# Scores of an attention unit ordered behind the transposes, not the value products, two units back

## The chip, the cores and the metric

The kernel runs on one core of a Trainium2 chip, as one launch. The metric is device time in microseconds (us): the median of several executions. A profiled execution gives, besides its time, the span from its first to its last instruction and a record of every instruction on every engine: PE (TensorE, matmuls), PEld (its weight loads), DVE (VectorE), ACT (ScalarE), POOL (GpSimd), SP (SyncE, which issues the weight DMAs).

## What is computed

Two transformer blocks follow one another, for one sequence of 512 tokens and 1024 channels, in float32. The first block is FFN, a mixer of dilated attention and a gated recurrence, FFN. The second block is run for two layers, l = 0 and 1: a *hybrid mixer*, then a dense FFN (l = 0) or a mixture of eight experts (l = 1). Only the hybrid mixer, "the second kind of mixer", is touched. Its core, cut to what matters:

```
z = h @ w_in                      # q (8 heads), 3 pairs of k/v (2 groups), gates, u, bg, cg
o_cmp, p_cmp = cmp_attention(q, kc_c, vc_c)       # 31 compressed keys
o_sel = sel_attention(q, ks, vs, idx)             # 512 tokens are 8 blocks of 64, all chosen: causal
o_win = win_attention(q, kw, vw)                  # window of 512: causal
o_attn = g[0] * o_cmp + g[1] * o_sel + g[2] * o_win
o_conv = bg * conv3(cg * u)
return concatenate([o_attn, o_conv]) @ w_o
```

With 512 tokens both `o_sel` and `o_win` are plain causal softmax attention, so a mixer has 8 heads times 2 such branches.

## The kernel before

Every product in float32 is made of three matmuls on halves: a value is cut into a high and a low half (hi, lo), and hi*hi, hi*lo and lo*hi are summed (`mm3`, lines 429 to 431). Weights arrive by DMA as `w_raw`; ACT makes the high half (line 276), DVE and POOL share the low half (lines 280 and 282).

**A mixer** (`mix2`) has a main stream on TensorE: three projections by tokens (`tok_out`), two compressions of keys and values (`compress_mm`), six convolution jobs (`conv_out`, each 48 matmuls of 512 columns), and the convolution's part of the output projection (`out_proj`, 96 matmuls of 512 columns). Attention runs beside it as side streams, and after `flow.flush()`, which lets all of them come to their end, the attention's part of the output projection (`out_proj` again, with `closing`) follows.

**A unit** is one head (n) and one branch (br), u = 2n + br, 16 in a mixer. Its stages (`unit`, lines 925 to 1000):

- *scores*: four tiles of queries, two matmuls each (lines 948 and 949) into one of two `ps_s` banks; DVE adds the causal bias and takes the extreme (958), ACT exponentiates (960), DVE makes reciprocal and gate (963, 965), POOL scales (968). The results lie in three of six `ex` buffers.
- *transposes*: ten 128x128 transposes (980) into three `ps_t` banks, each bank cut by ACT and DVE (417, 418) into two of eight `pr` buffers.
- *value products* (PV): twelve matmuls into the head's `ps_o`, of which there is one bank. Both units of a head and its compressed branch (1571) add into it; after that it is cut into the `tok` operand of the output projection (417, 418).

`prep(n)` stacks and transposes a head's queries into one of four `q` pairs; `compressed(n)` does the compressed branch.

**The order** comes from a planner, `Flow`, which runs while the program is built: streams yield (cost on TensorE, delay until the stream may go on) or an `Event` to wait for; the main stream goes on step by step, and before each step every side stream that is due gets its turn. A planner's wait is no semaphore on the chip: it only decides in which order instructions are written down. For a unit the yields are

```
                yield 2 * mm_us(n), lag[2]       # a tile of scores; mm_us(512) is 0.215, lag[2] is 0
        yield 0.0, lag[0]                        # 9.75 from the last score to the first transpose
            yield 0.11 * off / P, lag[2]         # transposes of a bank: 3, 4 and 3 of them
        self.flow.mark(turned)
        yield 0.0, lag[1]                        # 5.18 from the last transpose to the value products
        for ev in before_pv:
            yield ev
            yield 3 * mm_us((4 - j) * P), 0.0    # value products, 1.78 in all
```

What was written down is then scheduled by the framework (`TileContext(..., schedule_with_timeline_sim=True)`): the order written is a priority, instructions whose operands or buffers are not there yet are passed over, and each engine in the end runs its own queue strictly in order, with semaphores put in by the framework.

Before, the planner starts the scores of unit u when the value products of u - 2 are done, and `prep(n)` when the compressed branch of head n - 2 is done.

Of the kernel before, what the change touches and what calls it, by code (L numbers as in the profile page):

```python
# [371 lines left out]
class Build:  # L372
# [988 lines left out]
    def mix2(self, norm, l, after):  # L1361
# [3 lines left out]
        with tc.tile_pool(name="m2_c", bufs=1) as mc, tc.tile_pool(name="m2_r", bufs=1) as rp:  # L1365
# [25 lines left out]
            ev = {n: Event() for n in ("k0", "k1", "q0", "q1", "g0", "g1", "wp0", "wp1", "kst", "vst")}  # L1391
# [102 lines left out]
            prepped = [Event() for _ in range(8)]  # L1494
            unit_done = [Event() for _ in range(16)]
            turn = [Event() for _ in range(16)]
            cmp_done = [Event() for _ in range(8)]
# [3 lines left out]
            def prep(n):  # L1501
                hd = order[n]
                if n > 1:
                    yield cmp_done[n - 2]
                yield ev["q%d" % (n // 4)]
                d = self.stacked(q[n // 4][hd // 4][:, :, hd % 2 * 64:hd % 2 * 64 + 64])
                yield 0.0, 3.11
                hds[n]["q"] = self.r(rp, S, "q"), self.r(rp, S, "q")
                self.cut(hds[n]["q"][0], hds[n]["q"][1], self.stack_rows(d))
                yield 0.44, 0.0  # L1510
                flow.mark(prepped[n], 6.18)

            def attend(n, br):
                hd, u = order[n], 2 * n + br
                g = hd // 4
                wait = [prepped[n], ev["k%d" % br], ev["g0"]] + ([unit_done[u - 2]] if u > 1 else [])
                before = [unit_done[u - 1]] if br else []
                lead = None
                if br:
                    wait.append(ev["kst"])  # L1520
                    p = self.t(P)
                    hds[n]["p"] = p

                    def lead(i, sc):
                        c = slice(i * 32, i * 32 + 32)
                        nc.vector.tensor_tensor(p[:, c], sc, cmp_bias[:, c], ALU.add)
                        if i == 0:
                            flow.mark(scored[n], 0.3)

                yield from self.unit(rp, hds[n], lambda: keys[br][g], causal, gates[:, :, br * 8 + hd],  # L1530
                                     lambda j: (vals[br][0][:, j], vals[br][1][:, j]),
                                     br == 0, False, wait, [turn[u - 1]] if u else [], turn[u], before,
                                     unit_done[u], None, lead)

            def compressed(n):
# [43 lines left out]
            for n in range(8):  # L1579
                flow.spawn(prep(n), 10 + 2 * n)  # L1580
                flow.spawn(attend(n, 0), 10 + 2 * n)
                flow.spawn(attend(n, 1), 11 + 2 * n)
                flow.spawn(compressed(n), 11 + 2 * n)
# [725 lines left out]
```

## Time and profile before

| | us |
|---|---|
| three runs: median (lowest to highest) | 2613.47 (2603.94 to 2617.77) |
| the profiled execution | 2615.04 |
| its span, first to last instruction | 2613.4 |
| second kind of mixer, l = 0: first unit's scores to last unit's PV | 1145.3 to 1347.6 |
| the same, l = 1 | 1820.0 to 2022.5 |

The profiled execution's time is 1.6 us over its span, and 1.6 us over the median of the three runs. All times below are us from the start of the span. A matmul's row shows its own duration, which overlaps the next one's: the distance from start to start is what it costs in a full stream.

### The profile page before, as it was taken

The numbers are of one execution on the slowest core, as the hardware profiler recorded it, in microseconds if no ns is written. First come the engines' busy times: TensorE is split into PE (matmuls) and PEld (weight loads), VectorE is DVE, ScalarE is ACT, GpSimd is POOL, SyncE is SP. The second block draws the span as 40 slices with busy tenths as digits, with TensorE's granted clock in tenths as the row PEclk, the third lists the DMA queues.
The fourth block names the chain that finished last, engine by engine and source line by source line (L and its number), as shares of the span: only waits on it lengthen the run. The fifth ranks groups of instructions, "written<-read, shape, count | busy, mean of one in ns | idle before, by whom it ended". The sixth has DMA issues, their size and how long they took to land. (4 is left out here: it accounts for less than half of the span.)

```text
span 2613.4 us, 39953 instructions
## 1 busy us (share of the span) xinstructions
PE 2520.9 (96%) x14307; PEld 2177.7 (83%) x14307; DVE 1622.0 (62%) x3324; ACT 1200.1 (46%) x2230; POOL 865.9 (33%) x885
## 2 busy tenths in 40 slices
PE   8999999999999999999999999999999998999996
PEld 6888889898888887898888888879888896978885
DVE  5424455768754344686775323358777577899886
ACT  4222235564532222455544222225555376777763
POOL 4222232322122222433233222243322116677630
PEclk9999999998999999999999999999999898999997
DMA  5734432212122322241112232232311298799892
GB/s 179 173 117 125 123 125 82 65 50 65 33 97 74 112 97 73 92 135 65 57 41 81 82 104 97 77 110 93 101 57 43 82 322 313 249 372 324 313 346 88
DMA packets 103883, 342.06 MB, mean 131 GB/s; under 512 B 11966, under 2 KB 12782, under 8 KB 103680
## 3 DMA queue, kind: packets, MB, share of 16 engines
q1 hardware_dynamic: 95616, 311.58, 35.1%
q0 software_dynamic: 8064, 27.87, 4.0%
q8 instruction: 115, 1.88, 0.3%
q14 instruction: 88, 0.72, 0.1%
HBM read 316.59 MB, written 22.81 MB: 130 GB/s over the span
## 5 line engine op out<-in xcount | busy, mean ns | idle before, releaser
L282 POOL TENSOR_TENSOR w_lo<-w_raw,w_hi 128x224 fp32r<-128x224 f32 (+3 forms) x542 | 615.5, 1140 | 1173.4 <-ACT w_hi L276 1093.5
L276 ACT CAST w_hi<-w_raw 128x1024 fp32r<-128x1024 f32 (+3 forms) x615 | 598.9, 982 | 827.1 <-issue 233.8
L280 DVE TENSOR_TENSOR w_lo<-w_raw,w_hi 128x800 fp32r<-128x800 f32 (+5 forms) x616 | 662.0, 1086 | 275.3 <-ACT w_hi L276 267.9
L430 PE MATMUL ps_mm<-act_lo,w_hi 128*128 128x512 f32 (+1 forms) x784 | 303.1, 387 | 1.3 <-DVE act_lo L418 1.3
L429 PE MATMUL ps_mm<-act_hi,w_hi 128*128 128x512 f32 (+1 forms) x784 | 304.1, 388 | 0.3 <-ACT act_hi L417 0.3
L431 PE MATMUL ps_mm<-act_hi,w_lo 128*128 128x512 f32 (+1 forms) x784 | 302.5, 386 | 0.0
L429 PE MATMUL ps_s<-act_hi,w_hi 128*128 128x512 f32 (+1 forms) x456 | 174.6, 383 | 7.0 <-ACT w_hi L279 6.6
L431 PE MATMUL ps_s<-act_hi,w_lo 128*128 128x512 f32 (+1 forms) x456 | 173.7, 381 | 1.1 <-DVE w_lo L280 1.1
L430 PE MATMUL ps_s<-act_lo,w_hi 128*128 128x512 f32 (+1 forms) x456 | 174.2, 382 | 0.0
L968 POOL TENSOR_SCALAR ex<-ex,st 128x512 f32<-128x512 f32 (+3 forms) x160 | 92.1, 588 | 246.5 <-DVE st L965 146.5
L431 PEld LDWEIGHTS ps_mm<-act_hi,w_lo 128*128 128x128 f32 x784 | 148.7, 190 | 29.0
L430 PEld LDWEIGHTS ps_mm<-act_lo,w_hi 128*128 128x128 f32 x784 | 148.2, 189 | 29.0 <-DVE act_lo L418 1.6
L429 PEld LDWEIGHTS ps_mm<-act_hi,w_hi 128*128 128x128 f32 x784 | 147.9, 189 | 28.0 <-ACT act_hi L417 0.3
L429 PE MATMUL ps_mm<-w_hi,act_hi 128*128 128x256 f32 (+1 forms) x544 | 157.4, 289 | 9.9 <-DVE nat L1259 5.6
L431 PE MATMUL ps_mm<-w_hi,act_lo 128*128 128x256 f32 (+1 forms) x544 | 156.3, 287 | 0.2 <-DVE act_lo L634 0.2
L430 PE MATMUL ps_mm<-w_lo,act_hi 128*128 128x256 f32 (+1 forms) x544 | 155.9, 287 | 0.0
L960 ACT ACTIVATE ex<-ex,st 128x512 f32<-128x512 f32 (+3 forms) x160 | 89.5, 560 | 65.4 <-DVE st L958 65.0
L429 PEld LDWEIGHTS ps_mm<-w_hi,act_hi 128*128 128x128 f32 x544 | 104.2, 191 | 11.9 <-DVE nat L1259 6.1
L429 PEld LDWEIGHTS ps_s<-act_hi,w_hi 128*128 128x128 f32 x456 | 86.4, 190 | 24.8 <-ACT w_hi L279 6.6
L430 PEld LDWEIGHTS ps_mm<-w_lo,act_hi 128*128 128x128 f32 x544 | 104.1, 191 | 0.9 <-DVE w_lo L280 0.5
L431 PEld LDWEIGHTS ps_mm<-w_hi,act_lo 128*128 128x128 f32 x544 | 103.9, 191 | 0.9 <-DVE act_lo L634 0.5
L431 PEld LDWEIGHTS ps_s<-act_hi,w_lo 128*128 128x128 f32 x456 | 86.8, 190 | 19.7 <-DVE w_lo L280 1.9
(700 smaller groups left out, 6305.1 us busy)
## 6 DMA issues: line engine op xcount, KB each, us to landing
w_raw<-ffn_a SPq DMA_DIRECT2D x131, 512.0 KB, 3.6
w_raw<-moe_x SPq DMA_DIRECT2D x128, 512.0 KB, 5.8
w_raw<-moe_a SPq DMA_DIRECT2D x88, 512.0 KB, 6.0
w_raw<-ffn_b SPq DMA_DIRECT2D x48, 384.0 KB
w_raw<-ffn_b SPq DMA_DIRECT2D x48, 320.0 KB, 2.8
w_raw<-m_conv SPq DMA_DIRECT2D x24, 512.0 KB, 3.7
w_raw<-moe_b SPq DMA_DIRECT2D x32, 384.0 KB, 4.4
w_raw<-win_n SPq DMA_DIRECT2D x20, 512.0 KB, 4.0
```

The costliest lines, as they stand in the source:

```text
L276: self.late(self.nc.scalar.copy(hi, src))
L280: self.nc.vector.tensor_tensor(lo[:, :n - m], src[:, :n - m], hi[:, :n - m].bitcast(F32), ALU.subtract)
L282: self.nc.gpsimd.tensor_tensor(lo[:, n - m:], src[:, n - m:], hi[:, n - m:].bitcast(F32), ALU.subtract)
L429: mm(out, l[0], r[0], start=first, stop=False)
L430: mm(out, l[0], r[1], start=False, stop=False)
L431: mm(out, l[1], r[0], start=False, stop=last)
L960: nc.scalar.activation(s, s, AF.Exp, bias=st[:, o:o + 1], scale=-1.0, accum_out=st[:, 2 + o:3 + o])
L968: nc.gpsimd.tensor_scalar(ex[i], ex[i], st[:, 4 + o:5 + o], 1.0, ALU.mult, ALU.mult)
```

## The change

Four waits of the planner are altered, and nothing else; no instruction, tile, buffer count or DMA is added or taken away.

```
             def prep(n):
                 if n > 1:
-                    yield cmp_done[n - 2]
+                    yield turn[2 * n - 3]
...
-                wait = [prepped[n], ev["k%d" % br], ev["g0"]] + ([unit_done[u - 2]] if u > 1 else [])
-                before = [unit_done[u - 1]] if br else []
+                wait = [prepped[n], ev["k%d" % br], ev["g0"]] + ([turn[u - 2]] if u > 1 else [])
+                order_t = ([turn[u - 1]] if u else []) + ([unit_done[u - 2]] if u > 1 else [])
+                before = [unit_done[u - 1]] if br else [cmp_done[n - 1]] if n else []
...
-                                     br == 0, False, wait, [turn[u - 1]] if u else [], turn[u], before,
+                                     br == 0, False, wait, order_t, turn[u], before,
                                      unit_done[u], None, lead)
```

`turn[u]` is marked when the transposes of unit u are written, `unit_done[u]` after its value products, `cmp_done[n]` after the compressed branch of head n. So scores of u wait for the transposes of u - 2; transposes of u wait for those of u - 1, as before, and now also for the value products of u - 2; the first value products of a head wait for the compressed branch of the head before; and a head's queries are prepared once the second unit of head n - 2 is transposed.

## Rows read from the trace of the kernel before

**Rows 1.** The page's first part: busy time (share of the span) xinstructions
```profile
PE 2520.9 (96%) x14307; PEld 2177.7 (83%) x14307; DVE 1622.0 (62%) x3324; ACT 1200.1 (46%) x2230; POOL 865.9 (33%) x885
```

**Rows 2.** Stretches: length; PE, PEld, DVE, ACT, POOL busy us; clock, DMA, GB/s
```profile
1145.00:1327.00 182.00, 181.51 (x1078) 159.11 (x1077) 135.47 (x410) 97.38 (x240) 57.00 (x82) 1.00 0.23 74
1327.00:1349.00 22.00, 20.98 (x134) 18.18 (x133) 15.04 (x50) 12.25 (x32) 4.88 (x9) 1.00 0.08 25
...
2002.00:2024.00 22.00, 18.47 (x118) 15.61 (x116) 15.66 (x56) 12.24 (x32) 5.37 (x10) 1.00 0.09 30
```

**Rows 3.** Waits of PE, 1805 to 2025: total, times, longest
```profile
PE ps_o L429 <- DVE tok L418: 1.6, 1, 1.6
PE ps_t L1563 <- DVE c L1559: 1.1, 1, 1.1
PE ps_mm L429 <- DVE vl L418: 0.8, 1, 0.8
PE ps_mm L429 <- ACT tok L417: 0.7, 1, 0.7
```

**Rows 4.** Timeline of PE around 1325: start, us, instruction
```profile
1324.15 0.39 PE L429 MATMUL ps_mm<-act_hi,w_hi 128*128 128x512 f32 x1
1324.38 0.40 PE L430 MATMUL ps_mm<-act_lo,w_hi 128*128 128x512 f32 x1
...
1327.64 0.39 PE L429 MATMUL ps_mm<-tok,w_hi 128*128 128x512 f32 x1
...
1347.58 0.39 PE L1571 MATMUL ps_o<-c,vst 96*128 96x512 f32 x1
1348.64 0.50 PE L429 MATMUL ps_mm<-tok,w_hi 128*128 128x512 f32 x1 [0.67 <-ACT tok L417]
```

**Rows 5.** Timeline of PE: fourth unit's first scores, second unit's first value product
```profile
1178.25 0.50 PE L948 MATMUL ps_s<-k,q 128*128 128x512 f32 x1
...
1187.20 0.40 PE L429 MATMUL ps_o<-pr,vh 128*128 128x512 f32 x1
```

**Rows 6.** DVE, 1145 to 1345, by line: count, busy us, mean ns, idle before
```profile
L958 DVE CUSTOM_DVE_ANT_0 ex<-ps_s,c_causal 128x512 f32<-128x512 f32 (+1 forms) x64 | 30.3, 484 | 15.2 <-PE ps_s L949 10.0 <-PE ps_t L955 4.9
L418 DVE TENSOR_TENSOR pr<-ps_t,pr 128x384 fp32r<-128x384 f32 (+1 forms) x46 | 27.2, 595 | 7.1 <-ACT pr L417 7.0
L280 DVE TENSOR_TENSOR w_lo<-w_raw,w_hi 128x800 fp32r<-128x800 f32 x24 | 24.9, 1040 | 5.3 <-ACT w_hi L276 5.2
...
L1599 DVE SCALAR_TENSOR_TENSOR cv<-cu,c_m_taps,cv 128x510 f32<-128x510 f32 x4 | 3.2, 810 | 0.1
...
L1596 DVE TENSOR_SCALAR cv<-cu,c_m_taps 128x512 f32<-128x512 f32 x4 | 2.5, 615 | 0.1
```

**Rows 7.** Stretches with a fuller DVE; columns as in Rows 2
```profile
1125.00:1145.00 20.00, 18.19 (x149) 17.43 (x148) 19.38 (x39) 13.05 (x23) 6.99 (x7) 1.00 0.37 112
...
2300.00:2400.00 100.00, 96.31 (x505) 78.89 (x504) 91.59 (x105) 79.39 (x120) 76.85 (x68) 1.00 0.95 350
2400.00:2500.00 100.00, 99.48 (x656) 90.28 (x655) 92.30 (x136) 78.10 (x139) 62.09 (x64) 1.00 0.88 310
```

**Rows 8.** Timelines of DVE and POOL: low halves of weights
```profile
1240.70 0.99 DVE L280 TENSOR_TENSOR w_lo<-w_raw,w_hi 128x800 fp32r<-128x800 f32 x1 [1.82 <-ACT w_hi L276]
...
1252.09 1.46 DVE L280 TENSOR_TENSOR w_lo<-w_raw,w_hi 128x800 fp32r<-128x800 f32 x1
...
1240.74 1.48 POOL L282 TENSOR_TENSOR w_lo<-w_raw,w_hi 128x224 fp32r<-128x224 f32 x1 [0.87 <-ACT w_hi L276]
...
1251.87 0.84 POOL L282 TENSOR_TENSOR w_lo<-w_raw,w_hi 128x224 fp32r<-128x224 f32 x1 [1.12 <-ACT w_hi L276]
```

**Rows 9.** Stretches after the last unit, l = 1; columns as in Rows 2
```profile
2030.00:2035.00 5.00, 5.00 (x33) 4.69 (x33) 2.12 (x4) 0.00 (x0) 0.22 (x1) 0.76 0.33 108
2035.00:2040.00 5.00, 5.00 (x23) 4.55 (x23) 1.71 (x3) 1.29 (x4) 0.00 (x0) 0.50 0.00 0
2040.00:2045.00 5.00, 5.00 (x29) 4.29 (x28) 0.73 (x2) 0.00 (x0) 0.00 (x0) 0.72 0.00 0
```

## The prediction

> **What bounds the kernel now.** I read the page's first part, then stretches around the two hybrid mixers, then the waits of TensorE in them, and last the timeline where a wait stands.
>
> The first part says that TensorE is busy 96% of the span and no other engine comes near it [rows 1]. The change takes no instruction away, so it can only win back time in which TensorE stands still, and only inside the two mixers, about 2 x 202 us from the first unit's scores to the last unit's value products.
>
> In the body of a mixer, 1145 to 1327, TensorE is busy 181.5 of 182 us at full clock [rows 2]. As a busy share counts modelled ends, I checked the timeline: two matmuls of 512 columns start 0.23 us apart, though each is listed with 0.39 [rows 4]; 512 columns at 2.4 GHz are 0.213. The stream is closed. What is left lies in the tail, from the end of the convolution's part of the output projection to the end of the last unit: there TensorE is busy 20.98 of 22 us for l = 0 and 18.47 of 22 for l = 1 [rows 2]. So 1.02 + 3.53 = 4.55 us idle. Three waits make up 1.6 + 1.1 + 0.7 = 3.4 us of l = 1 (the listed 0.8 for `vl` lies before the first unit) [rows 3].
>
> The tail is short because the scheduler already fills it: at 1327.64 matmuls of the final projection (`tok`, heads that are done) run although two units are still to come [rows 4]. At the end nothing is left to fill with: from 1347.58 to 1348.64 the projection waits for the last head's cut, 1.06 us from start to start where 0.23 is the rule, of which the profile lists 0.67 as idle [rows 4]. So a listed gap hides some 0.16 us more (0.39 - 0.23). With about eight gaps in both tails that is 1.3, and the tails cost 4.55 + 1.3 = 5.8 us together.
>
> **The change, part by part.** All four waits are the planner's; no semaphore, instruction or DMA comes or goes. SP's queue, which carries only weights, is written in the main stream's order as before; POOL keeps its 64 scalings and its shares of the low halves.
>
> *Scores behind `turn[u - 2]`.* Before, two units pass through scores, 9.75, transposes, 5.18 and value products: 1.19 + 9.75 + 1.1 + 5.18 + 1.78 = 19.0 planner us for two, 9.5 for one. After, the loop is 1.19 + 9.75 + 1.1 = 12.0 for two, 6.0 for one. As a unit needs 1.19 + 1.1 + 1.78 = 4.1 of TensorE itself and the main stream moves in steps of 0.65 to 1.3, both come out longer. I played the planner's clock through for both orders with the yields in the code. Units 4 to 15 take 139 planner us before and 110 after (11.6 and 9.2 for one). The last unit ends 10.9 us behind the convolution's projection before, and 27 us ahead of it after. The chip ends the last unit 20 us behind that projection (1347.6 against 1327.4), so it lags the plan by some 9. With three times that lag it would still be in time after the change: I take it that both tails go, -5.8 us. The bounds are 0 (nothing moves on the chip) and -5.8.
>
> *The new waits before transposes and before a head's first value products.* At no cost. A unit's scores waited for `unit_done[u - 2]` before, so its later transposes did too. And as there is one `ps_o` bank, a head's first value product could never pass the cut of the head before. Nothing is queued behind them on an engine, since they only order the writing.
>
> *`prep` earlier.* Eight times a mixer one copy, four transposes, two cuts. They are hidden behind the same two heads as before; the fourth `q` pair is the limit. I put it at nothing; if a score had to wait for `q`, main matmuls would cover it, as they do now for every unit.
>
> *What a denser attention costs.* This is the term against the change. DVE is busy 135.5 + 15.0 = 150.5 us from 1145 to 1349 [rows 2]. Main-stream work in it is 24.9 (low halves) and 14.3 (five convolution groups, from 3.2 to 2.5 each) [rows 6]. That leaves 111 us, or 7.0 for each of 16 units; scores (30.3) and cuts (27.2) are its largest groups [rows 6]. In the planned 110 us, 12 units need 84, and five of six convolution jobs need ten halves of 1.04 and 5/6 of 14.3, 22 together: 106 of 110, 96%, where DVE now has 74%. The trace shows what TensorE does beside so full a DVE: 0.5 idle of 100 (2400 to 2500, DVE 92%), 3.7 of 100 (2300 to 2400, DVE 92%, fuller DMA), 1.8 of 20 (1125 to 1145, DVE 97%) [rows 7]. Over 2 x 110 us that is 1.1, 8.1 or 20 us. I take 1%, 2.2 us. Of the three stretches the mixer is nearest to 2400 to 2500, with ready weights and a main stream that fills; I double its price for the higher share.
>
> One more collision can grow. DVE's low half took 0.99 us at 1240.70 while POOL's, which began 0.04 later, took 1.48; at 1252.09 POOL had begun first with 0.84, and DVE took 1.46 [rows 8]. So about 0.5 us falls on the one that comes second.
>
> The Trainium skill, "SBUF — State Buffer", section "Who interferes with whom", says that a DVE instruction with two SBUF inputs and a GpSimd instruction that reads SBUF exclude each other for the whole instruction. These rows agree with it, and by that rule a denser DVE loses more to POOL.
>
> I add nothing for it, as the number of pairs stays the same; were every one of the 2 x 64 scalings to cost DVE 0.5 us, DVE would need 32 us more in each mixer, and the dear end above (20 us) would hold.
>
> **Sum**, against the profiled execution: 2615.0 - 5.8 + 2.2 = 2611.4. That execution lies 1.6 over the median, so the median to expect is 2609.8; I say 2610.
>
> **The rivals.**
>
> *The half clock goes too.* The three stretches of 5 us after 2030 have a granted clock of 0.76, 0.50 and 0.72, with TensorE busy without a gap [rows 9]. 0.76 is 2.4 us at 1.2 GHz, so it fell at 2032.6, ten us after the last unit, and (0.24 + 0.50 + 0.28) x 5 = 5.1 us of work are lost. Before that it stood idle 3.5 us in the tail [rows 2]. If the tail's gaps bring the fall, the time is 2604.7. Against it: between the tail and the fall lie some eight us of dense matmuls at full clock.
>
> *The change does nothing on the chip.* The order written is only a priority. Even now the fourth unit's scores start at 1178.25, nine us ahead of the value products of the second (1187.20) for which the planner makes them wait [rows 5]. If buffers (six `ex`, eight `pr`, one `ps_o`) set the pace, the tails stay: 2613.
>
> *Slower.* DVE becomes the bound in the dense part and the main stream's low halves, written later than the attention that now precedes them, come too late; TensorE waits for weights or for a `ps_mm` bank to be emptied. Place: the convolution jobs, 1170 to 1300 and 1845 to 1975. Price: the dear ends above, 8.1 to 20 us, less 5.8: 2616 to 2628. It turns the sign once TensorE idles over 5.8 / 220 = 2.6% of the dense stretch. Against it: DVE's longer waits now are short ones behind TensorE and ACT [rows 6], and the cut buffers hold two jobs of weights.
>
> *Overlap fills hidden room under the closed stream.* Weight loads are busy only 159.1 of 182 us [rows 2]. If the other 22.9 were room, three units at a time would find it: 2613.5 - 2 x 22.9 = 2568. Against it: the distance of 0.23 leaves no room for another matmul.
>
> The Trainium skill, "Perfetto Trace Analysis", section "Identifying the Most-Contended Engine", says to judge TensorE's headroom by the share of its weight loads, not by matmul busy time, and by that rule there are those 13%. The spacing in the timeline does not agree.
>
> **How the numbers follow.** Forecast (2603 to 2617) 45%; half clock gone too (2598 to 2609) 18%; nothing moves (2610 to 2617) 15%; slower by DVE (2614 to 2630) 20%; hidden room 2%. About 0.5%, 13 us, is what a measurement of this kernel can tell from no change; the three runs before spread over 13.8 us, so a median may move by some us by itself. Faster by over 0.5% (under 2600.4) needs the hidden room, or the lost clock regained with nothing paid to DVE and a lucky median: 15%. Slower by over 0.5% (over 2626.5) needs TensorE idle over (13 + 5.8) / 220 = 8.6% of the dense stretches: 11%. The same: 74%. The range 2599 to 2624 leaves out the hidden room, the upper half of the slow case and little else.
>
> **What would show it.** Right: the last unit ends before the convolution's projection in both mixers; the waits for `tok` and `c` in the tails are gone; scores of u start before the value products of u - 2 throughout; DVE is over 85% busy in the dense part and TensorE still over 98%. Wrong: `tok` matmuls still run between the last units; TensorE waits in the convolution jobs on `w_lo`, `ps_mm` or `pr`; or a stretch at half clock appears or vanishes, which moves the time by 3 to 7 us with no regard to the order.

## The result: 0.8% slower

The changed kernel takes 2633.24 us (median of 8 runs, 2626.33 to 2637.08). Beside it on the same chip the kernel before took 2611.51 (8 runs). The ratio is 1.0082, with an interval of 1.0068 to 1.0096. The prediction was 2610 with a range to 2624. The profiled execution took 2635.22 us, its span 2633.6, which is 20.2 more than before.

The page's first part of the kernel after has the same instructions and TensorE at 96% again, so it doesn't tell where the 20 us are [rows 1]:

```profile
PE 2534.0 (96%) x14307; PEld 2188.6 (83%) x14307; DVE 1622.8 (62%) x3324; ACT 1200.6 (46%) x2230; POOL 873.5 (33%) x885
```

From the first scores to the last product of the compressed branch a mixer took 202.3 and 202.5 us. Now it takes 214.4 (1146.1 to 1360.5) and 217.0 (1832.6 to 2049.6). That is +12.1 and +14.5. The first scores start 0.8 later, the work between the mixers is 0.3 shorter, and what follows the second mixer is 6.9 shorter: 12.1 + 14.5 + 0.8 - 0.3 - 6.9 = 20.2. The loss lies in the mixers. Stretches of the kernel after (columns as in [rows 2]):

```profile
1146.00:1314.00 168.00, 167.36 (x976) 145.73 (x975) 117.95 (x340) 82.84 (x199) 50.35 (x69) 1.00 0.24 79
1314.00:1340.00 26.00, 19.86 (x109) 17.10 (x108) 18.43 (x70) 15.18 (x42) 7.72 (x13) 0.87 0.06 21
1340.00:1361.00 21.00, 19.71 (x126) 16.83 (x125) 15.56 (x51) 11.49 (x33) 4.47 (x8) 1.00 0.00 1
...
1146.10:1360.50 214.40, 206.47 (x1206) 179.56 (x1204) 151.84 (x459) 109.40 (x271) 62.54 (x90) 0.98 0.19 64
1832.60:2049.60 217.00, 207.96 (x1190) 181.00 (x1188) 152.60 (x465) 109.12 (x271) 62.73 (x92) 0.96 0.19 65
...
1320.00:1325.00 5.00, 3.27 (x19) 2.97 (x19) 2.76 (x9) 1.74 (x5) 0.82 (x2) 0.79 0.01 3
...
1330.00:1335.00 5.00, 2.90 (x13) 1.75 (x11) 4.39 (x22) 3.74 (x13) 2.58 (x5) 1.00 0.00 0
1335.00:1340.00 5.00, 2.79 (x14) 2.79 (x15) 1.76 (x6) 1.86 (x5) 1.59 (x4) 0.66 0.00 0
```

The two mixers of the kernel before:

```profile
1145.30:1347.60 202.30, 201.46 (x1206) 176.68 (x1204) 149.82 (x459) 109.05 (x271) 61.58 (x91) 1.00 0.21 69
1820.00:2022.50 202.50, 198.83 (x1190) 174.17 (x1188) 150.72 (x466) 109.05 (x271) 62.01 (x91) 1.00 0.21 69
```

Up to 1314 TensorE is as full as before, and DVE is busy 70% (118 of 168). Then it starves. The convolution's projection, the filler, is through at 1314.0 (before 1327.4), but the last unit ends at 1360.5 (before 1347.6). TensorE is idle 7.9 us of the first mixer and 9.0 of the second, where it was 0.8 and 3.7. About the idle times the granted clock is lower: 0.79, 0.87 and 0.66 in three stretches of 5 us of the first mixer. There 7.1 us more idle time and up to 3.4 lost at the lower clock make 10.5 of the 12.1. In the second mixer it is 5.4 more idle and, by a granted clock of 0.96 over 217.0 us, up to 8.7 lost at the lower clock, together 14.1 of the 14.5.

The waits of TensorE in the second mixer, 1832 to 2050 (us in total, times, longest), beside [rows 3]:

```profile
PE ps_t L1564 <- DVE c L1560: 5.6, 2, 3.9
PE ps_o L429 <- ACT pr L417: 1.4, 1, 1.4
PE ps_o L430 <- DVE pr L418: 0.6, 2, 0.4
```

L1564 (L1563 before) is the four transposes of a head's compressed weights `c`, in the function `compressed`; below they are called the *flips*. The same wait, 5.6 us in two, stands in the first mixer.

Where the units fall behind can be read earlier, though nothing waits there. Timelines of POOL, DVE and PE in the kernel after around its fifth unit (u = 4: start, us, instruction):

```profile
1211.53 2.06 POOL L968 TENSOR_SCALAR ex<-ex,st 128x512 f32<-128x512 f32 x4 [2.91 <-DVE st L965]
...
1217.16 0.69 DVE L418 TENSOR_TENSOR q<-ps_t,q 128x512 fp32r<-128x512 f32 x1
...
1221.52 0.24 PE L948 MATMUL ps_s<-k,q 128*128 128x160 f32 x1
...
1225.69 0.39 PE L948 MATMUL ps_s<-k,q 128*128 128x512 f32 x1
...
1227.90 0.28 DVE L1560 TENSOR_TENSOR c<-t,c 128x128 fp32r<-128x128 f32 x1
...
1232.52 0.60 PE L1564 MATMUL ps_t<-c_ident,c 128*96 128x128 f32 x4
1232.95 0.93 PE L980 MATMUL ps_t<-c_ident,ex 128*128 128x128 f32 x7
...
1238.74 0.68 DVE L958 CUSTOM_DVE_ANT_0 ex<-ps_s,c_causal 128x512 f32<-128x512 f32 x1
```

The same in the kernel before:

```profile
1215.66 0.83 POOL L968 TENSOR_SCALAR ex<-ex,st 128x256 f32<-128x256 f32 x2 [1.29 <-DVE st L965]
...
1218.83 0.49 PE L980 MATMUL ps_t<-c_ident,ex 128*128 128x128 f32 x3
...
1235.21 0.60 PE L1563 MATMUL ps_t<-c_ident,c 128*96 128x128 f32 x4
1235.64 0.60 PE L980 MATMUL ps_t<-c_ident,ex 128*128 128x128 f32 x4
```

Before, the unit's scaled scores are there at 1216.5 and its transposes start at 1218.8. After, they are there at 1213.6, and the transposes start at 1233.0, right behind the flips of their head (1232.5), which needed a `c` that was ready at 1228.2; the last 4.3 us from there to the flips are not explained here. The seventh and ninth units (u = 6, 8) show the same: scaled at 1247.4 and 1284.3, flips at 1263.6 and 1297.9, transposes at 1264.5 and 1298.4. Before, only the odd unit stood behind the flips (1235.2, then 1235.6). One wait follows from it: the scores of u = 6 are made at 1225.69 and taken out of PSUM only at 1238.74, when the transposes of u = 4 free an `ex` buffer.

It is not that the three `ps_t` banks were full. The last reader ahead of the flips is the cut of the next queries, which ends at 1217.9 (the row of line 418); from then until the flips are loaded at 1232.3 the trace shows nothing that writes or reads any of the three. What holds the transposes is their place behind the flips.

The planner explains the order. The flips are due 4.1 planner us after the last tile of the odd unit's scores (`scored` is marked at tile 0, which is written last; 0.3 + 3.78), the even unit's transposes 9.75 after its own last tile. Replayed with the yields of the code, the plan before writes scores of u = 4 at 72 and of u = 5 at 80, the transposes of u = 4 at 84 and the flips at 86. After, both scores are written at 68 and 69, the flips at 76 and the transposes at 79. On the chip the odd unit's scores alone, one planner us from first to last tile, took 7.1 us (1214.4 to 1221.5), and `c` was ready another 6.7 behind the last tile (1228.2), not 4.1.

### The profile page after: what moved, and what is told of

Its sections match the earlier page's. It is cut to its first block, busy times and chain, and to the rows that moved or that the text cites. A ratio compares the mean times of both kernels' runs of the same rounds, so it can differ in the third digit from the quotient of the medians.

```text
span 2633.6 us, 39950 instructions
## 1 busy us (share of the span) xinstructions
PE 2534.0 (96%) x14307; PEld 2188.6 (83%) x14307; DVE 1622.8 (62%) x3324; ACT 1200.6 (46%) x2230; POOL 873.5 (33%) x885
## 5 line engine op out<-in xcount | busy, mean ns | idle before, releaser
L282 POOL TENSOR_TENSOR w_lo<-w_raw,w_hi 128x224 fp32r<-128x224 f32 (+3 forms) x542 | 625.3, 1159 | 1226.2 <-ACT w_hi L276 1157.9
L968 POOL TENSOR_SCALAR ex<-ex,st 128x512 f32<-128x512 f32 (+3 forms) x160 | 86.3, 552 | 214.4 <-DVE st L965 99.2
```

Of the source, the lines that this page charges most:

```text
L282: self.nc.gpsimd.tensor_tensor(lo[:, n - m:], src[:, n - m:], hi[:, n - m:].bitcast(F32), ALU.subtract)
L968: nc.gpsimd.tensor_scalar(ex[i], ex[i], st[:, 4 + o:5 + o], 1.0, ALU.mult, ALU.mult)
```

## Experiments

Theory F: the flips, written ahead of the even unit's transposes, are late on the chip and hold these up; they share three `ps_t` banks. Rival X: the six `ex` buffers, room for two units, are what three units lack. Rival P: the early `prep`. Theory D is the prediction's slow rival, a full DVE. From the fifth run on, F is widened to O: the banks go in the order in which their users are written, the query transposes of `prep` and the narrow compressed scores (line 954) included; Q stands for P. Each kernel was timed 5 to 12 times, in batches on different chips; the kernel before had medians of 2609.7 to 2611.8 us in them, and each ratio is to the one of its own batch. "Mixers" is from the first scores to the last product of the compressed branch in the profiled execution.

| run | us | ratio to before | mixers, us |
|---|---|---|---|
| after | 2633.24 | 1.0082 (1.0068 to 1.0096) | 214.4, 217.0 |
| e1 flips last | 2598.28 | 0.9957 (0.9941 to 0.9972) | 198.0, 198.1 |
| e2 before, flips first | 2634.58 | 1.0097 (1.0077 to 1.0116) | 215.5, 216.8 |
| e3 `ex` for three | 2624.62 | 1.0062 (1.0041 to 1.0083) | 211.4, 212.4 |
| e4 before, early `prep` | 2619.97 | 1.0036 (1.0023 to 1.0049) | 207.6, 207.9 |
| e5 `prep` back | 2631.73 | 1.0079 (1.0060 to 1.0098) | 213.0, 213.2 |
| e6 before, flips last | 2610.78 | 0.9999 (0.9989 to 1.0009) | 203.5, 201.7 |
| e7 flips last, `prep` back | 2608.04 | 0.9989 (0.9977 to 1.0000) | 203.6, 203.9 |
| e8 before, early `prep`, scores first | 2610.53 | 0.9996 (0.9986 to 1.0007) | 203.4, 203.2 |
| e9 flips of ready data | 2881.66 | (see e9) | 198.6, 198.5 |
| e10 flips between | 2600.08 | 0.9954 (0.9942 to 0.9967) | 196.6, 197.7 |
| e11 flips last, `ex` for three | 2605.43 | 0.9975 (0.9964 to 0.9985) | 200.9, 198.1 |

**e1: the changed kernel, flips written behind the transposes of both units.**

```
                 yield 0.0, 3.78
+                yield turn[2 * n + 1]
                 ps = self.psum("t")
```

> The changed kernel, with one more planner wait: the four transposes of a head's compressed branch (the flips) are written only after the transposes of the head's second unit. Theory F (flips first: the change made the planner write the flips ahead of the transposes of both units of the head, and these, drawing on the same three ps_t banks, cannot go before the flips, which wait for the compressed softmax): the transposes of units 4, 6 and 8 follow the end of their scaling by 2 to 5 us instead of 14 to 19, the last unit of l = 0 ends by 1348 instead of 1360, and the time falls to 2600 to 2615. Theory X (three units need nine ex buffers and there are six): the pace is set by ex, the last unit still ends after 1355, 2625 to 2636. Theory D (the slow rival of the prediction: DVE full, main stream starved): no change of this kind helps, 2625 to 2636.

The loss is gone and more: 35 us faster than the change, 0.43% faster than before. The transposes of u = 4 start at 1207.0 with POOL ending at 1207.1. Of the 17.7 us between the profiled spans 8.7 are the two mixers (not all of it gain, see *Both tails go* below). Another 6.8 lie ahead of the first mixer, in code that the change does not touch; between 600 and 800 us the granted clock was 0.97 in this execution and 0.94 in that of before.

**e2: the kernel before, with only the harm.** The units' transposes wait for `flipped[n]`, marked after the flips and their cut.

```
-    [turn[u - 1]] if u else [], turn[u], before,
+    ([turn[u - 1]] if u else []) + [flipped[n]], turn[u], before,
```

> The kernel before, with the suspected harm alone: the transposes of both units of a head are written only after the flips of the head's compressed branch; the four waits of the change are not made. Theory F: even units' transposes now stand behind the flips too, attention ends later than 1347 by 8 us or more, 2622 to 2645. Theory X and theory D: scores start as before, so ex and DVE are loaded as before, 2605 to 2618.

It loses as much as the change, with the old waits in all else. PE in e2 for u = 4, whose scores were scaled by 1226.3:

```profile
1242.89 0.60 PE L1564 MATMUL ps_t<-c_ident,c 128*96 128x128 f32 x4
1243.33 0.49 PE L980 MATMUL ps_t<-c_ident,ex 128*128 128x128 f32 x3
```

**e3: the changed kernel, with `ex` room for a third unit** (the tile of 256 columns in three buffers of its own; the space comes from smaller `pr` and `c` buffers).

> The changed kernel, with ex room for three units (six full buffers and three of 256 columns; paid for by cutting pr into three of 512 and five of 384 columns and the compressed branch's buffers into two of 384 and two of 512). Theory X: scores of unit 6 are taken out of PSUM as soon as they are made (first one at 1226 instead of 1239), 2600 to 2615. Theory F: the transposes of units 4, 6 and 8 still wait 14 to 19 us for the flips and the last unit ends after 1355, 2622 to 2636.

It wins back some of the loss: 8.6 of 22 us by the medians, 5 by the ratios, whose intervals overlap; its two profiled mixers are 7.6 us shorter than after the change. The scores of u = 6 are through at 1236.6, not 1243.4, but the transposes of u = 6 and 8 still stand behind the flips (flips 1261.0 and 1296.1, transposes 1261.9 and 1296.5). X has a part only as a consequence.

**e4: the kernel before, with the early `prep` alone** (`yield turn[2 * n - 3]` for `yield cmp_done[n - 2]`).

> The kernel before with one part of the change alone: a head's queries are prepared once the second unit of head n - 2 is transposed. All three theories: nothing, 2606 to 2617; a rival P, that the earlier copies, query transposes and cuts take ps_t banks and DVE time from the units, wants 2618 to 2635.

I had put this edit at nothing; alone it costs 10 us, as rival P had it, though e8 gives another reason than P. PE in e4, the sixth unit's (u = 5) scores and their narrow part for the compressed branch, which takes a `ps_t` bank:

```profile
1217.94 0.39 PE L948 MATMUL ps_s<-k,q 128*128 128x512 f32 x1
...
1229.79 0.26 PE L955 MATMUL ps_t<-k,q 128*128 128x32 f32 x1
```

and in the kernel before:

```profile
1216.18 0.26 PE L955 MATMUL ps_t<-k,q 128*128 128x32 f32 x1
...
1217.94 0.45 PE L948 MATMUL ps_s<-k,q 128*128 128x512 f32 x1
```

With the early `prep` the plan writes the transposes of u = 4 ahead of the scores of u = 5, and their narrow part runs 12 us behind the first of these scores. `c` is ready at 1238.7 (before 1230.6).

**e5: the changed kernel with `prep` back.**

> The changed kernel with one part undone: a head's queries are prepared behind the compressed branch of head n - 2 again, as before the change. Preparing early alone cost 10 us (2619.97) and lengthened the two mixers from 202 to 208 us each. Theory O (three ps_t banks are handed out in the order in which their users are written: unit transposes, flips of the compressed branch, query transposes, narrow compressed scores): by a replay of the planner the flips then stand ahead of the even unit's transposes in four heads of eight instead of six, so part of the loss goes: mixers of 205 to 212 us, 2614 to 2628. Theory Q (the early preparation is the loss, through the q buffers or DVE): all of it goes, mixers of 202 us, 2604 to 2613. Were the preparation without effect here: 2630 to 2637.

2631.73 is above what O was given and hardly below the change. My count there was off: by the replay the flips stand ahead of the even unit's transposes in four heads of the changed kernel (u = 4, 6, 8, 12) and in three of this one (4, 8, 12). The trace agrees with that, head for head: the transposes of u = 6 start at 1255.1, right after its scaling (1254.5); those of 4, 8 and 12 at 1239.7, 1298.2 and 1337.7, right behind flips at 1239.3, 1297.7 and 1336.9. In the changed kernel, `prep` is not the loss.

**e6: the kernel before, flips last.**

> The kernel before, with one wait more: the four transposes of a head's compressed branch (the flips) are written after the transposes of both its units. It has the old scores' wait and the old preparation, so no third unit overlaps. Theory O: before, the odd units' transposes came 4 to 9 us behind POOL's scaling, right behind the flips; that delay goes, and the mixers shrink from 202 to 199 to 201 us: 2603 to 2609. Rival, the overlap is what the late flips need to bring anything: mixers of 202 us as before, 2608 to 2613. Rival, all that the changed kernel with late flips gained (2598.28) comes from the flips: 198 us, 2596 to 2601.

Nothing changed; my forecast of 2603 to 2609 missed, and the first rival (mixers as before) came true. That an odd unit stands 4 to 9 us behind the flips cost nothing in the kernel before.

**e7: flips last and `prep` back.**

> The changed kernel with the flips written after the transposes of both units of the head, and with the preparation of queries back where it was. Theory O: with the flips late, an early or late preparation matters little, since neither holds a bank for long: mixers of 197 to 201 us like the 198 with the early one, 2595 to 2604. Theory Q: the early preparation still costs its 10 us in the version with late flips, so this one is faster by that much: 2586 to 2591. Rival, the overlap needs the early preparation, as scores wait for it: mixers of 202 us, 2605 to 2612.

The last rival came true: with `prep` back, e1's gain of 0.43% shrinks to 0.11%, hardly clear of none. A late `prep` holds up scores: those of u = 12 start at 1302.2, 26 us after the last of u = 10, where the even units before them are 13 to 15 us apart in this way (u = 8 to 10: 1254.2 to 1268.6). So overlap pays only with the early `prep`.

**e8: e4, and the even unit's transposes wait for the odd unit's scores** (`+ ([] if br else [scored[n]])`).

> The kernel before with the early preparation of queries, which alone cost 10 us, and one wait more: the even unit's transposes are written behind the first tile of the odd unit's scores, whose narrow part for the compressed branch takes a ps_t bank. In the run with the early preparation alone that narrow part of the sixth unit ran at 1229.8, behind the even unit's transposes, where it ran at 1216.2 in the kernel before, and the compressed branch was ready 8 us later. Theory O (banks in written order): the narrow part comes with the rest of its unit's scores again, and the loss goes: mixers of 202 to 204 us, 2607 to 2614. Theory Q (buffers of q, or the query transposes' own bank and cuts): the loss stays, mixers of 207 us or more, 2617 to 2624.

`scored` is marked with the last of the odd unit's four tiles; the narrow part belongs to the first, so it is written ahead of the even unit's transposes all the more. The 10 us are gone, so neither the `q` buffers nor the query transposes cost them.

**e9: the changed kernel, order untouched, flips that read the identity.**

```
-    pst[:, i * 96:(i + 1) * 96].bitcast(F32),
+    self.ident[:, :96],
```

> The changed kernel, order of writing untouched, but the four transposes of a head's compressed branch read the identity, which is always there, and not the head's compressed weights (so the compressed branch's share of the output is left out; its DVE, ACT and PE instructions all run). Theory O, that the units' transposes stand behind transposes whose operand is late: nothing is late any more, and the loss goes as it went with the flips written later: mixers of 197 to 200 us, 2594 to 2604. Rival, the loss is the place that the flips take in the ring of ps_t banks, their cut, or the written order of other things: it stays, mixers of 210 us or more, 2620 to 2635.

The mixers are what O says. Stretches of e9:

```profile
1143.70:1342.30 198.60, 197.39 (x1181) 172.93 (x1180) 150.92 (x460) 108.44 (x271) 59.54 (x90) 1.00 0.21 68
1815.80:2014.30 198.50, 197.99 (x1190) 173.71 (x1188) 150.82 (x465) 108.25 (x271) 60.17 (x92) 1.00 0.22 71
```

The order is the changed kernel's still. For u = 4 (first scalings through at 1207.3) the flips come first and the transposes right behind them, but both 14 us ahead of the `c` that the flips no longer read:

```profile
1210.05 0.60 PE L1564 MATMUL ps_t<-c_ident 128*96 128x128 f32 x4
1210.49 0.49 PE L980 MATMUL ps_t<-c_ident,ex 128*128 128x128 f32 x3
...
1224.57 0.29 DVE L1560 TENSOR_TENSOR c<-t,c 128x128 fp32r<-128x128 f32 x1
```

So the place of the flips in the order is harmless once their data is there. The total says nothing on the change: 864 us follow the second mixer, where the kernel before has 591. There the experts are chosen by values, which this run alters, and a loop over additional blocks has a count from that choice; that it is this loop was not tried.

**e10: flips between the two units' transposes** (`yield turn[2 * n]`).

> The changed kernel with the flips written between the transposes of the head's two units: behind those of the even unit, ahead of those of the odd one, as they stood in most heads of the kernel before. Theory O: only the odd unit waits for the compressed weights, which were ready 4 to 5 us behind that unit's own scaling where the flips came last; with three units in flight that is covered as it was before the change (where writing them last brought nothing, 2610.78): mixers of 198 to 203 us, 2597 to 2610. Rival, any wait of a unit's transposes for the compressed branch is paid in full when three overlap: 8 heads of 4 us in each mixer less what is covered, mixers of 206 us or more, 2614 or more.

As good as e1, so it is the even unit that must not stand behind the flips. Stretches of e10, its two mixers, their last 23 us, and what follows the second:

```profile
1146.20:1342.80 196.60, 196.25 (x1178) 172.68 (x1177) 146.99 (x457) 107.56 (x271) 62.28 (x89) 1.00 0.21 68
1816.80:2014.50 197.70, 196.60 (x1181) 173.03 (x1180) 150.55 (x466) 108.20 (x271) 65.36 (x91) 1.00 0.21 69
1320.00:1343.00 23.00, 23.00 (x128) 19.86 (x127) 13.42 (x40) 8.91 (x24) 5.82 (x8) 1.00 0.14 47
1992.00:2014.50 22.50, 22.50 (x127) 19.43 (x126) 15.44 (x47) 8.71 (x21) 7.54 (x10) 1.00 0.18 55
...
2025.00:2030.00 5.00, 5.00 (x28) 4.78 (x26) 0.98 (x2) 0.25 (x1) 0.00 (x0) 0.56 0.04 13
2030.00:2035.00 5.00, 5.00 (x27) 4.30 (x27) 1.16 (x3) 1.04 (x4) 0.00 (x0) 0.76 0.00 0
```

The tails have no gap left. A timeline of POOL and PE in e10 for u = 4 answers to the one of after: scaled at 1213.8, transposed from 1218.0.

```profile
1211.78 2.06 POOL L968 TENSOR_SCALAR ex<-ex,st 128x512 f32<-128x512 f32 x4 [2.91 <-DVE st L965]
...
1218.01 0.49 PE L980 MATMUL ps_t<-c_ident,ex 128*128 128x128 f32 x3
```

**e11: flips last and `ex` for three.**

> The changed kernel with the flips last, and room for a third unit's scores in the ex buffers (which alone took 8 us off the changed kernel). Theory O: the wait for ex was only a consequence of transposes that came late; with the flips last the sixth unit's scores were emptied without a gap (1219.6 to 1225.7), so the third room brings nothing more: mixers of 196 to 199 us, 2593 to 2602. Theory X, that ex is a bound of its own: another 4 us or more from each mixer, 2590 or less.

No further gain: it is 7 us behind e1 by the medians (the intervals of the ratios just overlap), and above O's 2602 too. X, which wanted 2590 or less, finds no support; that the smaller `pr` and `c` buffers, which pay for the room, hide a gain is not excluded.

## Why the prediction was wrong

*The step that failed* is the pace: "With three times that lag it would still be in time." I compared planned times of units and carried over one number for the chip's lag. The chip did not run the planned order late; a changed order made it run later. The last unit of the first mixer was to end 27 us ahead of the convolution's projection, and ended 46.5 behind it (1360.5 against 1314.0): the lag went from 9 to some 73 us, not to three times 9. My replay moved the compressed branch too, but I read off only the units, and the flips, whose order against the units' transposes is what turned, appear in no part of the working. Shown by harm alone (e2, +25 us), by cure through order (e1, e10) and by cure through readiness at the same order (e9). That the hold-up comes of `ps_t` banks being handed out in the order in which their users are written is argued from the code and the order of starts, and fits e4, e5 and e8. A want of banks it was not, as all three lay idle for 14 us before the flips of u = 4; a fourth bank was not tried.

*Both tails go, -5.8 us.* Right in size, but only with the flips in place: then the mixers shrink by 8.7 (e1) and 10.5 us (e10), and the tails run without a gap. Part of this is work that only moved: e10's two mixers hold 2359 matmuls, the kernel before's 2396, because fillers of the final projection (`tok`) now run after the last unit. Counted to the last `tok` matmul, the two stretches go from 469.4 us (1145.3 to 1372.0 and 1820.0 to 2062.8) to 463.2 (e1) and 460.8 (e10), 6.2 and 8.6 us less. The path differs from the plan as well: in e1 and e10 the last unit does not end ahead of the convolution's projection but 0.4 to 4.5 us behind it (1342.8 against 1342.4 in e10's first mixer). As the change stands, the mixers grow by 27.

*The price of a denser attention on DVE, +2.2.* Not seen. DVE did not come to the 96% of the plan: over the first mixer of e10, the densest, it is busy 147.0 of 196.6 us (75%). The work per mixer stays the same (149.8 us before). The rule of the Trainium skill on DVE and GpSimd excluding each other ("SBUF — State Buffer", "Who interferes with whom") would have made it dearer; no run here shows that. The two rows that I called in agreement [rows 8] show it in part only: the instruction that came second took 0.47 us longer for 0.62 of overlap (DVE, 1.46 against 0.99), and 0.64 for 0.95 (POOL, 1.48 against 0.84).

*The new waits at no cost.* In the replay the two added waits shift not one step: without them the planned times are the same to the hundredth. They weren't tried by themselves on the chip.

*`prep` at nothing.* Wrong alone (+10 us, e4), right within the change (e5). The reason that I gave was wrong as well: four `q` buffers, high and low halves, are two pairs, not four, here and in the section on the kernel. e8 shows that they were not the limit.

*The rivals.* Slower came true, at 1.0082 and above its 2616 to 2628, but not by its mechanism: it named a saturated DVE and TensorE waiting for weights at 1170 to 1300; TensorE is full there, and starves after 1314. Of the signs that I listed, `tok` matmuls between the last units and the last unit behind the convolution's projection came as the signs of "wrong". *The half clock goes too* fell: in e10 no gap is left in the tail, and it comes all the same; in e2, whose tails are as long as those of the change, it does not come within 35 us of the last unit. *Hidden room* (2568) fell: with three units truly overlapping the best is 2598. *The change does nothing* fell. (13 + 5.8) / 220 is 8.5%, not 8.6; nothing hangs on it.

## What to carry to other kernels

When streams share a ring of buffers and the order in which they are written is changed, list every user of the ring in the old and the new order, not only the stream that is moved, and ask of each one that moves forward whether its data will be there by then. A wait that never shows as a wait (the engine is full with other work) still costs, where the filler runs out. Put the step that depends on a long chain of small instructions behind those whose data is ready: one line here turned 0.8% slower into 0.4% faster than before.

## What was not expected of the hardware

The stretch at half clock (1.2 GHz) that follows the second mixer comes without listed idle time ahead of it. In e10 TensorE is busy 22.5 of the last 22.5 us of the mixer at full clock and without a gap from there on, and the clock is 0.56 between 2025 and 2030: it fell at about 2025.6, 11 us after the last unit, where it was ten before [rows 9]. Busy is not the same as full, though: from 2022.3 to 2025.1 TensorE ran one-row matmuls, 16 matmuls of 10 columns (`gate_w` by `xt`) and four transposes. Whether these bring the fall was not tried, and it is no fixed feature of the kernel: of the 13 profiled executions eight have a fall 10 to 13 us after the last unit, and five (e2, e3, e4, e8, e11) have none for 34 us; in e11 the clock is 1.00 from 2017.7 to 2040. In the kernel after, the clock falls within the tail as well, to 0.66 (1335 to 1340), next to stretches in which TensorE was idle for about two of five us.
